# First projection group multiplied with x times scale alone, alpha in 16 products, later modulation rows behind the q and k group

## The chip, the core and the metric

The kernel runs on one NeuronCore of a Trainium2 chip. Time is device time in microseconds (us) of one execution; each kernel is run several times and the median stands for it. One further execution was recorded by the hardware profiler; its own time and trace are what the sections below read. Engines: PE (TensorE, matrix products; PEld is its weight load), DVE (VectorE), ACT (ScalarE), POOL (GpSimd), SP (SyncE, which issues most DMAs).

## What is computed

One decoder block on a sequence of 1024 tokens of width 1024, all in float32. Of it, this matters here:

```python
mod = silu(c) @ w_ada + b_ada                  # (6*1024), six rows of 1024
shift1, scale1, gate1, shift2, scale2, gate2 = split(mod, 6)
h = rms_norm(x, norm1_w) * (1 + scale1) + shift1
proj = h @ w_in                                # q, k, v, r, a_lr, su, sv, g_a, g_b
z = a_lr @ w_alpha_up + b_alpha                # a_lr: 16 columns of proj
log_a = log_sigmoid(z) / 16
o = gla_chunked(q, k, v, log_a)                # 4 heads, gated linear attention
...
x = x + gate1 * (merged @ w_out)
h2 = rms_norm(x, norm2_w) * (1 + scale2) + shift2
x = x + gate2 * peer(h2)                       # 8 heads, top 16 of 16384 experts
```

rms_norm divides each token's row by the root of its mean square. As that divisor belongs to a row (token) and shift1 to a column (channel) of h, a product of h with a weight matrix can also be made as: row divisor times (x * norm1_w * (1 + scale1)) @ w, plus shift1 @ w.

## The kernel before

The sequence is worked in two halves of 512 tokens. In each half h stands transposed in SBUF (channels on partitions, eight blocks k of 128), and the columns of w_in are taken in groups of 512: V0 and V1 (the values), QK0 and QK1 (queries and keys of two heads each), then SV0, SV1, R0, R1, A0, A1, SU0, SU1, B0, B1. A group is eight steps k; one step multiplies four blocks of 128 into four PSUM banks (`mm`). To keep float32 accuracy, a factor is split in a high part rounded to the fast type (`wh`, `hTh`, by ACT) and the rest (`wl`, `hTl`, by DVE), and a product is three fast ones: high by high, high by low, low by high, 12 per step. A product of unsplit float32 tiles (`whole`, tiles `xt` and `wt`) takes four slower ones instead.

What comes first is written by hand in `first_group` (L1218): each instruction is put behind the one before on its engine by `put` (L1088), so PE, DVE, ACT and SP have a fixed order there. SP loads x transposed (2 MB), then for each pair of blocks (2 k and 2 k + 1) the shift and scale columns of w_ada (2 MB a pair, `AdaCols` L1117) and two weight tiles. The row norm comes from ACT squares of the x tiles, DVE sums, a product with ones, POOL's power (L1262), and a product that spreads it over the partitions (`dg`, `rrow`). The modulation columns of a pair are eight tiles times silu(c), summed on DVE (`adc`, 512 wide: shift and scale, 256 each), and a product with ones sums them over partitions (`close`); `store` adds the bias (`mod`) and makes `scol` = (1 + scale) * norm1_w. Then ACT and DVE make hTh, the whole h block and hTl, and PE multiplies block ka split and kb whole. `alpha` (L1303) makes the 16 columns of a_lr in three products a block, 24 in all; four heads' decay products follow (L1483), with ACT's Abs, Exp and Ln and a scan on DVE (L1576). Products with ones or iota (`keep_warm`) fill PE's waits at the start.

All later groups go through `stream` (L1398), which loads and splits weights ahead (`weights_ahead`, four split pairs and five loaded tiles at most), and after each step pumps queues of side work at given rates (`step`, L1047). Queue `qa` holds the modulation rows for gate1, scale2, shift2 and gate2 (`ada_row` L1161): eight loads of 512 KB each and eight DVE sums of width 1024 (`adacc`), and a product. They start with V1. Outside the hand-ordered part, a scheduler that works on a simulated timeline decides how these streams are interleaved on each engine.

The second half computes h in `x_prep` and `h_split`, runs the same groups, and beside them the expert rows of the first half, gathered by POOL (`direct_rows`); the expert mixer for the rest ends the program.

Of the kernel before, what the change touches and what calls it, by code (L numbers as in the profile page):

```python
# [17 lines left out]
P = 128  # L18
# [29 lines left out]
RD = 0.62  # L48
UVC = 4
# [18 lines left out]
DIRECT = ((3,), (), (), ())  # L68
WARM = 10
YA = True  # L70
VV = (0, 1)
# [10 lines left out]
def block_kernel(ctx: ExitStack, tc: tile.TileContext, x, xT, cT, w_ada, b_ada, b_adaT, n1T, w_inp, w_alr,  # L82
# [972 lines left out]
    with ExitStack() as pa:  # L1055
# [23 lines left out]
        wal = b2.tile([RANK, 512], F32, name="wal", tag="b2")  # L1079
        walr = b2.tile([P, KD, RANK], F32, name="walr", tag="b2")  # L1080
        wst = s1.tile([P, 8, P], F32, name="wst")
        walr_h = g1.tile([P, KD, RANK], F32R, name="walr_h")
        walr_l = g1.tile([P, KD, RANK], F32R, name="walr_l")
        wal_h = g1.tile([RANK, 512], F32R, name="wal_h")
        wal_l = g1.tile([RANK, 512], F32R, name="wal_l")
        tail = {}

        def put(eng, fn, *args, **kw):  # L1088
            with tc.issue_after(tail[eng]) if eng in tail else nullcontext():
                tail[eng] = getattr(getattr(nc, eng), fn)(*args, **kw).ins  # L1090

# [13 lines left out]
        def ada_acc(c):  # L1105
            acc = t4("adacc")
            for k in range(KD):
                wt = t4("wada")
                nc.sync.dma_start(wt, w_ada[k * P:(k + 1) * P, c * D:(c + 1) * D])
                if k == 0:  # L1110
                    with tc.issue_after(hlast[1]):
                        nc.vector.tensor_scalar(acc, wt, sc[:, 0:1], None, op0=OP.mult)
# [4 lines left out]
        class AdaCols:  # L1117
            def __init__(self, kp):
                w2 = 2 * P
                self.kp, self.direct = kp, DIRECT[kp]  # L1120
                self.chain = [q for q in range(KD) if q not in self.direct]
                self.acc = gl.tile([P, 2, w2], F32, name="adc", bufs=3)
                self.ps = auxt([P, 2, 2])
                self.wa = []
                for q in range(0, KD, 2):
                    wa = t4("wada").rearrange("p (a c f) -> p a c f", a=2, c=2)
                    src = w_ada[q * P:(q + 2) * P, :].rearrange("(a p) n -> p a n", p=P)
                    for c in range(2):
                        put("sync", "dma_start", wa[:, :, c], src[:, :, c * D + kp * w2:c * D + (kp + 1) * w2])
                    self.wa += [wa[:, 0], wa[:, 1]]  # L1130
# [87 lines left out]
        def first_group(src, evac, aps):  # L1218
# [27 lines left out]
            for k in range(KD):  # L1246
                sq = rowp.tile([P, HALF], F32, name="sq", tag="row") if k else acc
                put("scalar", "activation", sq, xts[k], AF.Square)
                if 0 < k < KD - 1:
                    keep_warm(sq[:, 0:256])  # L1250
# [659 lines left out]
```

## Time and profile before

| | us |
|---|---|
| median of 3 runs | 1421.45 |
| lowest and highest | 1417.21, 1423.58 |
| profiled execution, its own time | 1415.31 |
| its span in the trace | 1413.3 |
| first product of V0 | 22.8 |
| first product of V1 | 58.25 |
| first product of QK0 | 85.99 |

The span runs from the first to the last recorded instruction; the execution's own time has about 2 us more. A profile row of a timeline gives start, length, engine, line, operation, tiles written and read, count, and in brackets the idle time of the engine before it with what ended it. A row of windows gives, for a stretch, the busy time of PE, PEld, DVE, ACT and POOL, then PE's granted clock as a share of 2.4 GHz, the busy share of the 16 DMA engines, and GB/s. Most instructions of the hand-ordered part stand at L1090, the line in `put`.

### The profile page before, as it was taken

The page shows a single profiled execution, that of the slowest core. Times are in us where ns is not written, and L with a number is a line of the kernel's source. Part 1 is how long each engine was busy: PE and PEld are TensorE (multiplying, and loading weights), DVE is VectorE, ACT ScalarE, POOL GpSimd, SP SyncE. Part 2 cuts the span into 40 slices and gives each one's busy share as a digit, 9 for nine tenths or more (in the row PEclk, how much of TensorE's full clock was granted, in tenths as well). Part 3 has the DMA queues.
Part 4 walks back from the last instruction along what each step waited for, and adds up shares of the span by engine and source line. Part 5 has one row for each costly group of instructions (what it writes and reads, how often), then busy time and mean ns, then how long its engine had stood idle before and what let it go on. Part 6 is the DMA issues. An engine that isn't in the chain of part 4 may idle for free.

```text
span 1413.3 us, 19480 instructions
## 1 busy us (share of the span) xinstructions
PE 1341.5 (95%) x5998; PEld 1030.9 (73%) x5998; DVE 1078.9 (76%) x3073; ACT 697.7 (49%) x1560; POOL 293.8 (21%) x271
## 2 busy tenths in 40 slices
PE   8999999999999899998989999999989999789996
PEld 6678877888888887676767888887768886445553
DVE  7785777434468678898879887779889877799785
ACT  4454343333345465475434566556546554545542
POOL 0100001000000121332443143311121133443321
PEclk9999999999999999999999999999999999999998
DMA  9753553332257475767687798897687668897984
GB/s 327 257 205 112 187 177 128 98 98 82 95 180 269 159 275 172 244 219 258 197 297 272 243 338 335 319 336 266 217 298 280 213 246 323 339 385 310 391 295 175
DMA packets 118243, 339.75 MB, mean 240 GB/s; under 512 B 14745, under 2 KB 24217, under 8 KB 106098
## 3 DMA queue, kind: packets, MB, share of 16 engines
q0 software_dynamic: 31488, 163.85, 31.5%
q1 hardware_dynamic: 69296, 129.24, 27.1%
q10 hardware_dynamic: 17346, 45.34, 8.9%
q8 instruction: 48, 0.79, 0.2%
q14 instruction: 65, 0.53, 0.1%
HBM read 314.15 MB, written 24.23 MB: 239 GB/s over the span
## 4 chain that ended last, share of the span: by engine, by line
PE 34%; DMA 7%; DVE 7%; issue 6%; ACT 2%; POOL 1%; DVEq 0%; ACTq 0%; POOLq 0%
PE acc L608 6%; PE mm L183 5%; PE mm L184 5%; PE mm L186 5%; DMA uvd<-in_down_dram,dix 3%; PE mm L189 2%; DMA uv<-in_tab_dram,dix 2%; PE mm L190 2%; PE mm L191 2%; DVE uv L582 1%; PE hps L580 1%; PE hps L581 1%; PE acc L628 1%; PE acc L627 1%; DMA uv<-in_tab_dram,ix 1%
## 5 line engine op out<-in xcount | busy, mean ns | idle before, releaser
L1385 ACT ACTIVATE wh<-wt 128x512 fp32r<-128x512 f32 x344 | 212.5, 627 | 284.0 <-PE mm L184 126.9
L1387 DVE TENSOR_TENSOR wl<-wt,wh 128x512 fp32r<-128x512 f32 x344 | 231.5, 685 | 125.8 <-PE mm L186 62.5
L183 PE MATMUL mm<-wh,hTh 128*128 128x512 f32 x648 | 255.7, 395 | 1.5 <-ACT wh L1385 1.5
L184 PE MATMUL mm<-wh,hTl 128*128 128x512 f32 x648 | 253.8, 392 | 0.0
L186 PE MATMUL mm<-wl,hTh 128*128 128x512 f32 x648 | 204.1, 397 | 2.4 <-DVE wl L1387 2.4
L183 PEld LDWEIGHTS mm<-wh,hTh 128*128 128x128 f32 x648 | 121.7, 188 | 30.6 <-issue 3.1
L186 PEld LDWEIGHTS mm<-wl,hTh 128*128 128x128 f32 x648 | 120.6, 188 | 30.3 <-DVE wl L1387 4.4
L184 PEld LDWEIGHTS mm<-wh,hTl 128*128 128x128 f32 x648 | 121.7, 188 | 25.8 <-issue 0.4
L527 POOL DMA_INDIRECT uv<-in_tab_dram,ix x74 | 82.5, 1114 | 274.0 <-ACT ix L559 134.0
L183 PE MATMUL mm<-hTh,wh 128*128 128x512 f32 x240 | 95.6, 398 | 0.0
L184 PE MATMUL mm<-hTl,wh 128*128 128x512 f32 x240 | 94.8, 395 | 0.0
L582 DVE SCALAR_TENSOR_TENSOR uv<-uv,hps 128x512 f32<-128x512 f32 x112 | 74.9, 680 | 22.9 <-DMA uv<-in_tab_dram,ix 16.4
L189 PE MATMUL mm<-wh,hTh 128*128 128x512 f32 x216 | 85.4, 403 | 1.9 <-ACT vt L1451 1.6
L190 PE MATMUL mm<-wl,hTh 128*128 128x512 f32 x216 | 86.2, 399 | 0.0
L191 PE MATMUL mm<-wh,hTl 128*128 128x512 f32 x216 | 85.8, 397 | 0.0
L189 PE MATMUL mm<-hTh,wh 128*128 128x256 f32 (+1 forms) x208 | 70.2, 340 | 7.8 <-DVE q L1521 5.7
L754 POOL DMA_INDIRECT uvd<-in_down_dram,dix x32 | 39.0, 1218 | 161.2 <-DVE ts L361 48.0
L186 PE MATMUL mm<-hTh,wl 128*128 128x512 f32 x240 | 71.4, 398 | 0.1
L190 PE MATMUL mm<-hTl,wh 128*128 128x256 f32 (+1 forms) x208 | 68.5, 331 | 3.0 <-DVE hTl L175 3.0
L620 DVE SCALAR_TENSOR_TENSOR vl<-uv,r,vh 128x512 fp32r<-128x512 f32 x82 | 60.1, 745 | 11.5 <-ACT vh L619 5.8
L191 PE MATMUL mm<-hTh,wl 128*128 128x256 f32 (+1 forms) x208 | 67.5, 332 | 0.0
L608 PE MATMUL acc<-uv,W 128*128 128x512 f32 x132 | 63.4, 602 | 2.3 <-ACT W L597 1.8
(957 smaller groups left out, 2896.1 us busy)
## 6 DMA issues: line engine op xcount, KB each, us to landing
wt<-in_w_inp_dram SPq DMA_DIRECT2D x224, 256.0 KB, 3.9
wt<-in_w_qp_dram SPq DMA_DIRECT2D x72, 256.0 KB, 3.9
wada<-in_w_ada_dram SPq DMA_DIRECT2D x32, 512.0 KB, 4.8
wt<-in_w_outp_dram SPq DMA_DIRECT2D x56, 256.0 KB, 3.4
wada<-in_w_ada_dram SPq DMA_DIRECT2D x32, 256.0 KB, 5.9
s_d<-so ACTq DMA_DIRECT2D x28, 256.0 KB, 5.9
xr<-in_x_dram ACTq DMA_DIRECT2D x8, 512.0 KB, 4.3
x_d<-x ACTq DMA_DIRECT2D x8, 512.0 KB, 5.1
```

The costliest lines, as they stand in the source:

```text
L183: nc.tensor.matmul(ps, lh, rh, start=False, stop=False)
L184: nc.tensor.matmul(ps, *((lh, rl) if feat else (ll, rh)), start=False, stop=False)
L186: nc.tensor.matmul(ps, *((ll, rh) if feat else (lh, rl)), start=False, stop=False)
L189: nc.tensor.matmul(ps, lh, rh, start=first, stop=False)
L190: nc.tensor.matmul(ps, lh, rl, start=False, stop=False)
L191: return nc.tensor.matmul(ps, ll, rh, start=False, stop=last).ins
L527: nc.gpsimd.indirect_dma_start(out=dst[:], out_offset=None, in_=src, in_offset=off)
L582: nc.vector.scalar_tensor_tensor(uv[0][:, sl], uv[0][:, sl], 1.0, hps, op0=OP.mult, op1=OP.mult, accum_out=r[:, 2 + n:3 + n])
L608: ins = nc.tensor.matmul(acc[:, sl], W, v[:, sl], start=first, stop=last).ins
L620: nc.vector.scalar_tensor_tensor(vl, v, r[:, 5:6], vh.bitcast(F32), op0=OP.mult, op1=OP.subtract)
L1385: nc.scalar.activation(wh, wt, AF.Identity)
L1387: nc.vector.tensor_tensor(wl, wt, wh.bitcast(F32), op=OP.subtract)
```

## The change

The first two groups of the first half become one hand-ordered part, `first_groups`. V0 is multiplied from x times `scol` alone: no norm, no shift. Scale columns come pair by pair (256 wide, four steps q), from a new input `w_asc` that is laid out so that a partition's piece is 4 KB; block 2q is multiplied whole, block 2q + 1 split. The row norm comes from x loaded by rows (`xb`, another 2 MB) and enters as a factor when V0's banks are copied out (`ev_v0`). The shift's part of V0 is made later: DVE sums V0's kept weight tiles times the shift columns (`shift_rows`, tile `so`), one product with ones sums it over partitions (`shift_sum`), and DVE adds it to the four value tiles (`shift_add`), at steps 1 to 7 of QK0. The shift columns come in two parts of 512 (`w_ash`); the first is needed to start V1, the second for V1's fifth block. V1 is multiplied with the complete h: `turn` brings the norm into the scaled x, `split_h` adds the shift and splits.

Alpha takes high and low weights as 32 columns of one tile (`walr2`), so a block needs two products instead of three, in both halves; it is made in V1 instead of V0. Two heads' decay follows V1, the other two stand behind QK0's first step, and ACT's Exp and Ln with them. The modulation rows start with QK1 at rates 1.0 (QK1), 1.25 (SV0, SV1), 0 (R0), 0.5 (R1), 1.0 (A0, A1). The tiles of x, V0's weights and rows of x stand in buffers of later tiles: V0's weights in the `row` buffers and in `wst`, so the loads of glw, lnw, lnb and wst on ACT's queue wait for the shift rows.

```diff
         def ada_acc(c):
-            acc = t4("adacc")
+            acc, wts = t4("adacc"), []
+
+            def load(k):
+                wts.append(t4("wada"))
+                nc.sync.dma_start(wts[k], w_ada[k * P:(k + 1) * P, (c - 2) * D:(c - 1) * D])
...
+        def alpha(aps, k, emit):
+            hi = aps, walr2[:, k], hTh[:, k], k == 0, k == KD - 1
+            lo = aps[:RANK], walr2[:, k, :RANK], hTl[:, k], False, False
+            for o, w, h, first, last in (lo, hi) if k == KD - 1 else (hi, lo):
+                ins = emit("tensor", "matmul", o, w, h, start=first, stop=last)
...
+            scs = [load_scale(0, v4)]
+            load_x(0, 1)
+            load_w(0, 1, whole=False)
+            scs.append(load_scale(1, v4))
+            load_x(2, 3)
+            load_w(2, 3)
+            scs.append(load_scale(2, b4))
+            load_x(4, 5)
+            load_w(4, 5)
...
+            def scaled(dst, k):
+                put("scalar", "activation", dst, xts[k], AF.Identity, scale=scol[:, k:k + 1])
...
+            def norm():
+                rstd = sm_p.tile([P, BH], F32, name="rstd")
+                rstd0.append(rstd)
+                put("vector", "tensor_scalar", rstd, ss, 1.0 / D, EPS, op0=OP.mult, op1=OP.add)
+                nc.gpsimd.tensor_tensor(rstd, rstd, mhalf[:, :BH], op=OP.pow)
...
+            def turn(k):
+                if k % 2:
+                    put("vector", "scalar_tensor_tensor", xts[k], xts[k], scol[:, k:k + 1], rrow, op0=OP.mult, op1=OP.mult)
+                else:
+                    put("vector", "tensor_tensor", xts[k], xts[k], rrow, op=OP.mult)
...
+            for q in range(4):
+                ka, kb = 2 * q, 2 * q + 1
+                nps, _, add, close = channel_sums(scs[q + 1], [], 2 * P) if q < 3 else channel_sums(shs[0], [], 512)
+                whole(pss, ka)
+                if q == 3:
+                    squares(2)
+                add(1)
+                if q < 3:
+                    nwh = high(wts[kb + 2])
+                    if q == 2:
+                        squares(0)
+                    add(KD)
+                    if q:
+                        scaled_low(kb)
+                    nwl = low(wts[kb + 2], nwh)
+                else:
+                    add(2)
+                    norm()
+                    scaled_low(kb)
+                    add(2)
+                    norm_rows(norm_spread())
+                    add(KD)
+                cut = (8, 4, 4, 12)[q]
+                order = by_bank if q == 3 else by_part
+                products(pss, kb, wh, wl, order[:cut])
+                close()
+                products(pss, kb, wh, wl, order[cut:])
...
+                if q < 3:
+                    store_scale(nps, q + 1)
+                    scaled(xts[kb + 1], kb + 1)
+                    scaled(hTh[:, kb + 2], kb + 2)
...
             for k in range(KD):
...
+                    turn(k)
+                    nwh = high(w1[k])
+                split_h(k)
+                if k:
+                    nwl = low(w1[k], nwh)
...
+                if k < 4:
+                    add(2)
+                order = by_bank if k in (0, KD - 1) else by_part
+                products(pss1, k, nwh, nwl, order[:8])
+                if k == 3:
+                    close()
+                products(pss1, k, nwh, nwl, order[8:])
...
+                group(w_inp[G_QK0], ev_qk(0), True, post={0: later_decays, **late_shift}, hold=hold)
+                for c, r in ((2, 0), (4, 1), (3, 2), (5, 3)):
+                    qa.add(ada_row(c, r))
...
+            rate["a"] = RSV
...
+            for gid, ev, ra in ((G_R0, ev_r(0), 0.0), (G_R1, ev_r(1), 0.5), (G_A0, ev_a(0), 1.0), (G_A1, ev_a(1), 1.0)):
+                rate["a"] = ra
```

PE, ahead of the first products and through the first pair, before (tile `xt` is x, `aux` and `gaux` are PSUM banks for side products):

```order
L1090 MATMUL aux<-dg,ones 128x512
L1090 MATMUL gaux<-iota,ones 128x256 x3
L1090 MATMUL aux<-ones,adc 128x1 x4
L1090 MATMUL gaux<-iota,ones 128x256 x2
L1090 MATMUL mm<-wh,hTh 128x512 x4
L1090 MATMUL mm<-wl,hTh 128x512 x4
L1090 MATMUL mm<-wh,hTl 128x512 x4
L1090 MATMUL mm<-wt,xt 128x512 x4
```

and with the change, at the same place (`w_235` holds weight blocks 0 and 1):

```order
L1088 MATMUL aux<-sc,wada 128x1 x8
L1088 MATMUL aux<-ones,adc 128x1 x2
L1088 MATMUL gaux<-iota,ones 128x256
L1088 MATMUL mm<-w_235,xt 128x512 x4
L1088 MATMUL mm<-wh,hTh 128x512 x4
L1088 MATMUL mm<-wl,hTh 128x512 x4
```

and in the last pair of V0 (`wst` holds weight blocks 6 and 7):

```order
L1088 MATMUL mm<-wh,hTl 128x512 x4
L1088 MATMUL mm<-wst,xt 128x512 x4
L1088 MATMUL aux<-dg,ones 128x512
L1088 MATMUL mm<-wh,hTh 128x512
L1088 MATMUL mm<-wl,hTh 128x512
```

The spread of the norm (`aux<-dg,ones`) stood ahead of all products; now it stands between the last pair's whole and split products, and the first accumulating product follows the first pair's two scale columns.

DVE in the last pair of V0 and up to V1's first block, with the change (`adc` are shift sums, `rstd` the norm, `dg` its diagonal):

```order
L1088 SCALAR_TENSOR_TENSOR adc<-wada,sc,adc 128x512 x2
L1088 TENSOR_SCALAR rstd<-ss 128x4
L1088 SCALAR_TENSOR_TENSOR hTl<-xt,scol,hTh 128x512
L1088 SCALAR_TENSOR_TENSOR adc<-wada,sc,adc 128x512 x2
L1088 TENSOR_TENSOR dg<-ident,rstd 128x512
L1088 SCALAR_TENSOR_TENSOR adc<-wada,sc,adc 128x512 x3
L1088 TENSOR_TENSOR xt<-xt,rrow 128x512
L1088 TENSOR_TENSOR mod<-aux,badat 128x4
```

Before, DVE had the norm at the very start:

```order
L1090 TENSOR_TENSOR sqa<-sqa,sq 128x512 x7
L1090 SCALAR_TENSOR_TENSOR adc<-wada,sc,adc 128x512
L1090 TENSOR_SCALAR rstd<-aux 128x4
L1090 SCALAR_TENSOR_TENSOR adc<-wada,sc,adc 128x512 x2
L1090 TENSOR_TENSOR dg<-ident,rstd 128x512
```

Norm and diagonal moved behind the first shift sums, whose tiles SP loads after all of V0's.

ACT during QK0, with the change (`vt` the value tiles, `za` the decays):

```order
L1564 ACTIVATE vt<-mm 128x512 x3
L452 DMA glw<-in_gla_w_dram 128x1024
L1564 ACTIVATE vt<-mm 128x512
L1497 ACTIVATE wh<-wt 128x512
L1088 ACTIVATE za<-gaux,balt 128x512 x2
L452 DMA lnw<-in_ln_w_dram 128x1024
L1497 ACTIVATE wh<-wt 128x512
L452 DMA lnb<-in_ln_b_dram 128x1024
L1088 ACTIVATE za<-gaux,balt 128x512 x2
L1609 ACTIVATE za<-za 128x512 x4
```

The three row loads stand among V1's copies and the decays of QK0's time; before they were issued during V0, ahead of these.

More of the change, by code (lines that the diff above doesn't have):

```diff
@@ L1161, in ada_row, with mod_products @@
+        def mod_products(ps, wa, rows, direct):
+            w = wa[0].shape[1] // P
+            for r in rows:
+                for j in range(w):
+                    put("tensor", "matmul", ps[:, j:j + 1], wa[r][:, j * P:(j + 1) * P], sc[:, r:r + 1],
+                        start=r == direct[0] and j == 0, stop=len(direct) == KD and r == direct[-1] and j == w - 1)
         def ada_row(c, r):
@@ new lines, in low, with whole, parts, products @@
+            def low(w, wh):
+                wl = wsp.tile([P, 512], F32R, name="wl")
+                put("vector", "tensor_tensor", wl, w, wh.bitcast(F32), op=OP.subtract)
+                return wl
+            def whole(pss, k):
+                for i, cs in enumerate(cuts):
+                    put("tensor", "matmul", pss[i], xts[k][:, cs], wts[k], start=k == 0, stop=False)
+            def parts(k, wh, wl):
+                return (hTh[:, k], wh), (hTh[:, k], wl), (hTl[:, k], wh)
+            def products(pss, k, wh, wl, todo):
+                for n, i in todo:
+                    a, w = parts(k, wh, wl)[n]
+                    put("tensor", "matmul", pss[i], a[:, cuts[i]], w, start=k == 0 and n == 0, stop=k == KD - 1 and n == 2)
@@ new lines, in first_groups @@
+            keep_warm(ones, WARM)
+            ps, prod, add, close = channel_sums(scs[0], [0, 1, 2, 3], 2 * P)
+            prod([0, 1, 2, 3])
+            add(KD)
+            close()
+            store_scale(ps, 0)
+            keep_warm(iota)
+            pss = [mm.tile([P, 512], F32, name="mm", tag="mm") for _ in range(4)]
+            scaled(xts[0], 0)
+            wh = high(wts[1])
+            scaled(hTh[:, 1], 1)
+            wl = low(wts[1], wh)
+            scaled_low(1)
+            xb, shs = [], []
@@ L1246, in first_group @@
+            split_const(walr, walr2[:, :, :RANK], walr2[:, :, RANK:])
+            keep0.extend(wts)
+            nps, _, add, close = channel_sums(shs[1], [], 512)
+            pss1 = [mm.tile([P, 512], F32, name="mm", tag="mm") for _ in range(4)]
             for k in range(KD):
[L1247 to L1250, printed above, removed]
@@ L1472, in block_kernel, with decays @@
+            if hf == NHALF - 1:
+                qdir.add(direct_rows(t4, range(DIR)))
+            aps = gauxt([2 * RANK, HALF])
+            last_z = []
+            def decays():
+                for fn, kw in ((AF.Exp, {"scale": -1.0}), (AF.Ln, {"bias": 1.0})):
+                    with tc.issue_after(zi[0]):
+                        for za in zas:
+                            zi[:] = [nc.scalar.activation(za, za, fn, **kw).ins]
+                zlast[:] = [zi[0]]
             alh = t2("alh", F32R)
```

437 lines of the change are left out of this document (229 added, 208 removed).

## The prediction

> **What bounds the kernel now.** I read the page first, then windows of ten microseconds, then the timelines of PE, DVE and ACT for the first 110 us, which is where the change stands.
>
> ```profile
> span 1413.3 us, 19480 instructions
> ...
> PE 1341.5 (95%) x5998; PEld 1030.9 (73%) x5998; DVE 1078.9 (76%) x3073; ACT 697.7 (49%) x1560; POOL 293.8 (21%) x271
> ```
> ```profile
> 30.00:40.00 10.00, 9.20 (x38) 5.51 (x38) 9.15 (x17) 4.29 (x6) 0.00 (x0) 1.00 1.06 332
> ...
> 300.00:310.00 10.00, 10.00 (x46) 8.29 (x45) 3.83 (x6) 3.04 (x6) 0.00 (x0) 1.00 0.24 79
> ```
> ```profile
> 100.00:420.00 320.00, 317.87 (x1475) 260.77 (x1474) 178.66 (x304) 113.48 (x213) 9.12 (x5) 1.00 0.39 130
> 420.00:740.00 320.00, 297.17 (x1470) 243.85 (x1469) 262.16 (x824) 169.32 (x334) 89.27 (x70) 0.98 0.68 231
> ```
>
> In the windows the columns are busy PE, weight load, DVE, ACT, POOL, then granted clock, DMA share and GB/s. From 100 to 420 us PE is busy 317.87 of 320 us: whatever PE gains before 100 us goes through that stretch undiminished. Before 60 us PE is not the bound, DVE is (9.15 of 10). The PE timeline shows its pace (start, length, engine, line, tiles, idle before):
>
> ```profile
> 22.79 1.20 PE L1090 MATMUL mm<-wh,hTh 128*128 128x512 f32 x4 [0.33 <-ACT hTh L1090]
> ...
> 25.64 3.59 PE L1090 MATMUL mm<-wt,xt 128*128 128x512 f32 x8
> 28.68 0.79 PE L1090 MATMUL gaux<-hTh,walr_h 128*16 128x512 f32 x1
> ...
> 30.21 1.05 PE L1090 MATMUL aux<-ones,adc 128*128 128x1 f32 x8 [0.28 <-DVE adc L1090]
> ...
> 41.92 1.19 PE L1090 MATMUL mm<-wh,hTh 128*128 128x512 f32 x4 [0.57 <-ACT hTh L1090]
> ...
> 51.28 1.20 PE L1090 MATMUL mm<-wh,hTh 128*128 128x512 f32 x4 [0.58 <-ACT hTh L1090]
> ...
> 58.02 0.39 PE L1090 MATMUL gaux<-hTh,walr_l 128*16 128x512 f32 x1
> 58.25 0.39 PE L189 MATMUL mm<-wh,hTh 128*128 128x512 f32 x1
> ...
> 84.18 1.88 PE L1171 MATMUL aux<-adacc,ones 128*1 128x512 f32 x4
> 85.99 0.50 PE L189 MATMUL mm<-hTh,wh 128*128 128x512 f32 x1
> ```
>
> The first product of V0 starts at 22.79, pairs follow every 9.36 us (41.92 to 51.28), V0 with alpha ends at 58.25, V1 with the four decay products at 84.18, and QK0 starts at 85.99 behind a modulation row's 1.88 us. Twelve split products take 2.85 us (22.79 to 25.64), so one takes 0.23; four unsplit ones take 3.04 (25.64 to 28.68), and closing a pair's column sums (30.21, eight passes) 0.9.
>
> **The change, part by part.**
>
> **Start.** Norm and shift leave the path; what is left is one scale column pair.
>
> ```profile
> 0.79 4.38 SPq L1090 DMA_DIRECT2D xt<-in_xT_dram  x8
> ...
> xt<-in_xT_dram SPq DMA_DIRECT2D x8, 256.0 KB, 3.8
> ```
> ```profile
> L1607 DVE SCALAR_TENSOR_TENSOR ot<-ot,rso,glw 128x256 f32<-128x256 f32 x32 | 13.4, 474 | 0.1
> ```
> ```profile
> L1090 ACT ACTIVATE adc<-wada,sc 128x512 f32<-128x512 f32 x4 | 2.9, 716 | 1.6 <-DMA wada<-in_w_ada_dram 1.6
> ```
> ```profile
> 26.26 3.90 DVE L1090 SCALAR_TENSOR_TENSOR adc<-wada,sc,adc 128x512 f32<-128x512 f32 x5
> ```
> ```profile
> 31.69 0.81 ACT L1090 ACTIVATE hTh<-xt,mod,scol 128x512 fp32r<-128x512 f32 x1 [4.51 <-DVE scol L1090]
> ```
>
> Issued at 0.79 and landing in 3.8, the first scale tile is there at about 4.6, the second (512 KB more) at 5.2. A sum over 512 columns that needs the one before takes 0.78 (3.90 by 5). At 256 columns the trace has no such chain: it lies between 0.40, half of that, and 0.78; I take 0.51, nearest to the 0.474 that one such instruction lasts. So: ACT's first sum 0.5 (0.716 at twice the width), three DVE sums 1.5, closing products 0.5 (half of the 0.9), bias and scale 0.4, scaling x 0.75 (the 0.81 row without its bias), hand-offs 0.2: the first product at **9.1** instead of 22.8.
>
> **Pairs.** A pair now goes round one chain: scaling x and its high part 1.5, first sum 0.5, seven sums 3.6, two DVE instructions put between the sums and the scale (hTl, wl; below) 1.3, bias and scale 0.3: **7.2 us**, above PE's 3.04 + 2.72 + 0.5. Pair 3 starts at 9.1 + 3 × 7.2 = 30.7, not 51.28: 20.6 us ahead.
>
> **What is given back before V1.** In pair 3 PE does its unsplit products (to 33.8), then stands at the row-norm product, which the code puts ahead of the split ones.
>
> ```profile
> L1198 ACT ACTIVATE xb<-xb 128x1024 f32<-128x1024 f32 x4 | 4.2, 1056 | 2.7 <-DMA xb<-in_x_dram 2.7
> ```
> ```profile
> 13.14 1.51 POOL L1262 TENSOR_TENSOR rstd<-rstd,mhalf 128x4 f32<-128x4 f32 x1 [10.45 <-DVE rstd L1090]
> ```
>
> ACT: hTh to 31.5, two squares of 1.06 to 33.6, the first shift sum to 34.3. DVE: two shift sums, queued ahead of the norm, to 35.9; POOL's power to 37.5, beside which DVE has two more shift sums queued, to 38.0; the diagonal to 38.7. So PE is idle **4.9 us**. Then 0.76 for the spread, 2.72 split products, 0.9 closing the shift sums, 0.2 its store, 0.75 hTh: V1's first product at 44.4, against 58.25.
>
> This needs 12.9 MB landed by about 37 us (scales 4.2, x and its rows 4.2, V0's weights 2.1, two small loads 0.3, shifts 2.1):
>
> ```profile
> 28.00:30.00 2.00, 1.93 (x6) 0.48 (x4) 1.93 (x3) 0.00 (x0) 0.00 (x0) 1.00 1.10 355
> ...
> 70.00:72.00 2.00, 2.00 (x10) 1.67 (x9) 2.00 (x3) 0.63 (x1) 0.00 (x0) 1.00 1.02 408
> 72.00:74.00 2.00, 2.00 (x10) 1.65 (x10) 2.00 (x4) 0.00 (x0) 0.00 (x0) 1.00 1.03 414
> ```
>
> Rows of 1 KB moved at 355 GB/s, 4 KB rows beside weights at 408 to 414. The new tensors are read in 4 KB rows, x and some weights in 2 KB; I take 10.0 MB at 400 and 2.9 at 355, 33.2 us, from 2.5 on: the last shift tile is there at 36, just in time. At 355 throughout it is 39, and V1 starts 1.3 us later. The Trainium skill ("DMA: Bandwidth & Descriptors", Specifications) sets HBM's limit for a core near 358 GB/s. The rows at 408 and 414 say otherwise for stretches of 2 us; by the page the sum would be those 1.3 us worse.
>
> **V1.**
>
> ```profile
> 97.83 1.27 DVE L1387 TENSOR_TENSOR wl<-wt,wh 128x512 fp32r<-128x512 f32 x2
> ```
>
> At some 0.63 for a 512-column DVE instruction (two in 1.27), each of V1's first four rows costs DVE a turn, hTl, wl and two shift sums, 3.3 us, with a wait for ACT's hTh (0.72) inside, so about 3.9, more than PE's 2.72 + 0.45 of alpha. After the fourth stand the second shift columns' closing (0.9), their store, splitting the decay weights (1.0), a turn and hTh, 2.9 us in all before PE goes on. Rows five to eight run near PE's pace, 3.3. With two heads' decay products (six, 1.4): 15.6 + 2.9 + 13.1 + 1.4 = 33.0 us, to **77.4**. Before, 58.25 to 84.18 held all four heads' decay.
>
> **QK0.**
>
> ```profile
> 78.18 1.15 ACT L1493 ACTIVATE za<-za 128x512 f32<-128x512 f32 x2
> ...
> 80.90 1.28 ACT L1496 ACT_TABLE_LOAD   x1
> ```
> ```profile
> 87.07 1.22 DVE L1576 TENSOR_TENSOR_SCAN G<-smask,za 128x512 f32<-128x512 f32 x1
> ```
> ```profile
> L1114 DVE SCALAR_TENSOR_TENSOR adacc<-wada,sc,adacc 128x1024 f32<-128x1024 f32 x28 | 35.8, 1280 | 16.5 <-DMA wada<-in_w_ada_dram 16.4
> ```
>
> Add the other two decays (six products, 1.4) and the shift's column sum 0.76: 79.5, against 85.99 − 1.88 = 84.1 (the modulation row only moves). Lead 4.6 us. Eight shift rows (5.2 us) and four additions (2.5) on DVE are hidden by QK0's 21.8 us of PE; eight modulation sums of 1.28 leave it. On ACT four row loads now wait for tiles that these shift rows release, with the decay's Exp and Ln and the weight splits queued behind; three to four split weights are ahead, so I take 0; without that cover it is the second rival.
>
> **Modulation rows.** 32 sums on DVE and their loads go behind QK0 and into the gates. The 300:310 row has DVE at 3.83 of 10 there: nothing.
>
> **Alpha** in the second half: 8 products of 0.23, **1.8 us**, if PE is the limit there (297 of 320 busy): between 0 and 1.8, I take all.
>
> **The clock** is the term that I cannot settle.
>
> ```profile
> 12.00:14.00 2.00, 2.00 (x15) 1.95 (x14) 1.54 (x3) 0.20 (x1) 0.86 (x1) 0.78 1.10 347
> 14.00:16.00 2.00, 2.00 (x6) 1.64 (x6) 1.52 (x3) 0.00 (x0) 0.65 (x1) 0.50 1.08 366
> ...
> 18.00:20.00 2.00, 2.00 (x5) 1.21 (x5) 0.12 (x2) 1.19 (x3) 0.00 (x0) 0.51 1.10 347
> ...
> 642.00:644.00 2.00, 0.00 (x0) 0.00 (x0) 2.00 (x9) 1.62 (x3) 0.87 (x1) 1.00 1.02 392
> 644.00:646.00 2.00, 1.02 (x3) 0.86 (x4) 2.00 (x7) 1.51 (x3) 0.28 (x1) 0.65 1.03 407
> 646.00:648.00 2.00, 2.00 (x6) 1.61 (x5) 2.00 (x7) 0.77 (x2) 0.00 (x0) 0.50 1.03 408
> 648.00:650.00 2.00, 2.00 (x10) 1.60 (x10) 2.00 (x8) 0.02 (x1) 0.00 (x0) 1.00 0.89 344
> ```
>
> After some four microseconds with little on PE the grant fell to 0.50 (1.2 GHz); about 3 us of products then went at that level, a loss of 1.5. At the kernel's start it stayed there from 13 to 20, a loss near 3.5. The change has two such places: the one-column products ahead of the first pair, and the 4.9 us at the norm. Between 0 and 5.2 us; I take 2.9. The Trainium skill ("TensorE: Matmul & The Clock Gate", What's actually happening) calls the throttled state the default that activity releases, and the 644 to 648 rows agree; by it both places start slow, 2.3 us worse than my value.
>
> **Sum.** 4.6 − 2.9 + 1.8 = 3.5 us. The profiled execution, 1415.31 with a span of 1413.3, becomes 1411.8; it lies 6.1 under the median of the runs, 1421.45, so the median becomes **1418.0**.
>
> **Rivals.**
>
> *The whole front comes through.* If 256-column sums run at 0.40, a pair takes 6.4 and pair 3 starts at 28.3; if the norm's wait then shrinks to 2 us, V1 starts near 39 and, at PE's own 25.4 + 1.4, ends near 66 to 68, with the clock high. Lead 11 or so, with alpha 13: 1408.5. For it speaks that PE had 20.6 us in hand at pair 3; against it stand DVE's sums queued ahead of the norm.
>
> *ACT stands at its row loads (slower).* If shift rows run late, ACT sits in front of Exp and Ln. Then eight of them at 0.55 and two table changes of 1.3, 7 us, come after the last shift row instead of beside QK0, and the scans (4 × 1.2) behind them; QK0's fifth and later weights wait too. 7 + 4.9 less some 3 of cover, 9 us: 1427. It decides once ACT waits longer than the 5 us of split weights ahead. Against it: DVE frees the tiles within 10 us of V1's end.
>
> *Nothing arrives.* The second half waits for gathers:
>
> ```profile
> 592.48 5.93 DMA uvd<-in_down_dram,dix
> ```
>
> These are issued from results of the first half, so they move with it; but if the altered order of instructions lengthens a wait there by the same 3 us, 1421.5.
>
> **How the numbers follow.** Forecast (1412 to 1424, a small gain or none) 0.53; whole front 0.27; ACT's loads or slow clock throughout 0.13; nothing 0.07. 0.5% is 7.1 us, about what a measurement of this kernel tells from no change. Faster by more: 0.27, same 0.60, slower 0.13. The range takes in most of the first rival and the slower one: 1408.5 to 1427.
>
> **What would show it.** Right: PE's first accumulating product near 9, pair starts 7.2 apart, a PE wait of 4 to 6 us for `dg`, V1's rows 0 to 3 about 4 us apart with DVE releasing PE, QK0 starting 2 to 5 us earlier than 85.99 less 1.88, low clock grants near 10 and 40 us. Wrong: pairs at 6 us, no wait at the norm, or ACT idle at a row load in QK0 for over 5 us; also any change of over 4 us between 100 us and the end that the start doesn't explain.

## The result: 1.1% slower

| | before | after |
|---|---|---|
| median of the runs, us | 1421.41 (4 runs, 1417.21 to 1423.58) | 1437.95 (4 runs, 1431.43 to 1439.08) |
| ratio | | 1.0108, 95% interval 1.0075 to 1.0141 |
| profiled execution, us | 1415.31 | 1431.43 |

The page of the changed kernel, its span and busy times:

```profile
span 1429.6 us, 19379 instructions
...
PE 1338.7 (94%) x5952; PEld 1027.3 (72%) x5952; DVE 1085.0 (76%) x3094; ACT 694.2 (49%) x1561; POOL 291.5 (20%) x270
```

PE has 2.8 us less to do than before and the span is 16.3 us longer: PE stands 90.9 us instead of 71.8. Where? First the front, the PE timeline of the changed kernel (start, length, engine, line, tiles, count, idle before):

```profile
10.22 4.79 PE L1088 MATMUL mm<-w,xt 128*128 128x512 f32 x8 [0.28 <-ACT xt L1088]
...
18.87 3.70 PE L1088 MATMUL mm<-w,xt 128*128 128x512 f32 x8 [0.40 <-ACT xt L1088]
...
26.00 3.60 PE L1088 MATMUL mm<-w,xt 128*128 128x512 f32 x8
...
40.83 2.05 PE L1088 MATMUL aux<-dg,ones 128*128 128x512 f32 x2 [4.32 <-DVE dg L1088]
41.89 1.42 PE L1088 MATMUL mm<-wh,hTh 128*128 128x512 f32 x1
...
47.26 0.95 PE L1088 MATMUL aux<-ones,adc 128*128 128x1 f32 x8
49.39 0.50 PE L1088 MATMUL mm<-wh,hTh 128*128 128x512 f32 x1 [1.18 <-ACT hTh L1088]
...
83.22 0.51 PE L188 MATMUL mm<-hTh,wh 128*128 128x512 f32 x1
```

The pairs, the wait for `dg` and the stages stand where the prediction had them, each somewhat late; QK0 starts at 83.22. Six decay products and the shift's sum (1.4 + 0.76) are still to come, so this stands for 85.4, against 84.1 before: the front loses 1.3 us. (That alone is within one execution's scatter: e13 below has before's front, and QK0 started at 83.52 in it, not at 85.99.) Then the copies of two later groups on ACT, before: the last of the first half (`sg`, group B1) and the last of the second half's query groups (`qt`); what follows is the stretch that ends the program.

```profile
395.55 0.60 ACT L1633 ACTIVATE sg<-mm 128x512 f32<-128x512 f32 x1
...
1209.03 0.59 ACT L1749 ACTIVATE qt<-mm 128x512 f32<-128x512 f32 x1
```

The same with the change (the fourth of the four merged `qt` copies starts at 1217.7):

```profile
401.68 0.60 ACT L1798 ACTIVATE sg<-mm 128x512 f32<-128x512 f32 x1
...
1215.68 2.67 ACT L1916 ACTIVATE qt<-mm 128x512 f32<-128x512 f32 x4 [0.29 <-PE mm L190]
```

So the 16.3 us arise in three places: **6.1** in the first half (1.3 of them ahead of QK0, 4.8 behind), **2.6** from there to the last query group, although alpha saves time there, and **7.6** in the last stretch (211.9 us instead of 204.3), where the edit changes nothing. Two thirds of the loss stand behind the first half, where the change's one edit is alpha, a saving.

### The profile page after: what moved, and what is told of

It reads as the page before. It is cut to its first block, busy times and chain, and to the rows that moved or that the text cites. A ratio compares the mean times of both kernels' runs of the same rounds, so it can differ in the third digit from the quotient of the medians.

```text
span 1429.6 us, 19379 instructions
## 1 busy us (share of the span) xinstructions
PE 1338.7 (94%) x5952; PEld 1027.3 (72%) x5952; DVE 1085.0 (76%) x3094; ACT 694.2 (49%) x1561; POOL 291.5 (20%) x270
## 5 line engine op out<-in xcount | busy, mean ns | idle before, releaser
L1497 ACT ACTIVATE wh<-wt 128x512 fp32r<-128x512 f32 x336 | 207.8, 627 | 280.8 <-PE mm L183 116.2
L1499 DVE TENSOR_TENSOR wl<-wt,wh 128x512 fp32r<-128x512 f32 x336 | 227.2, 689 | 109.2 <-ACT wh L1497 58.1
L182 PE MATMUL mm<-wh,hTh 128*128 128x512 f32 x624 | 246.0, 394 | 2.1 <-ACT wh L1497 2.1
L183 PE MATMUL mm<-wh,hTl 128*128 128x512 f32 x624 | 245.7, 394 | 0.0
L185 PE MATMUL mm<-wl,hTh 128*128 128x512 f32 x624 | 194.5, 395 | 2.2 <-DVE wl L1499 2.2
L182 PEld LDWEIGHTS mm<-wh,hTh 128*128 128x128 f32 x624 | 117.4, 188 | 28.8 <-ACT wh L1497 3.1
L185 PEld LDWEIGHTS mm<-wl,hTh 128*128 128x128 f32 x624 | 116.0, 188 | 29.6 <-DVE wl L1499 3.0
L183 PEld LDWEIGHTS mm<-wh,hTl 128*128 128x128 f32 x624 | 117.2, 188 | 25.1 <-issue 0.9
L188 PE MATMUL mm<-wh,hTh 128*128 128x512 f32 x208 | 84.0, 410 | 4.7 <-DVE x L1886 2.1
L190 PE MATMUL mm<-wh,hTl 128*128 128x512 f32 x208 | 81.8, 393 | 0.0
L189 PE MATMUL mm<-wl,hTh 128*128 128x512 f32 x208 | 81.7, 393 | 0.0
```

What stands on the lines that cost most here:

```text
L182: nc.tensor.matmul(ps, lh, rh, start=False, stop=False)
L183: nc.tensor.matmul(ps, *((lh, rl) if feat else (ll, rh)), start=False, stop=False)
L185: nc.tensor.matmul(ps, *((ll, rh) if feat else (lh, rl)), start=False, stop=False)
L188: nc.tensor.matmul(ps, lh, rh, start=first, stop=False)
L189: nc.tensor.matmul(ps, lh, rl, start=False, stop=False)
L190: return nc.tensor.matmul(ps, ll, rh, start=False, stop=last).ins
```

## The experiments

The table holds all kernels: end of the first half (start of its last `sg` copy), from there to the last `qt` copy, the last stretch (three parts of the profiled span), and the ratio of the runs to before's with its interval. "Order" names the second half's order of instructions: the scheduler makes one of a few, which I compared row by row on each engine. X is before's, Z the changed kernel's; "own" was seen once. "Shift" is explained at the thirteenth run.

| run | order | shift | first half | to last query | last stretch | ratio (95%) |
|---|---|---|---|---|---|---|
| before | X | no | 395.6 | 813.4 | 204.3 | 1 |
| after | Z | yes | 401.7 | 816.0 | 211.9 | 1.0108 (1.0075 to 1.0141) |
| e1 | Y | no | 398.2 | 810.7 | 202.6 | 1.0028 (1.0000 to 1.0056) |
| e2 | Y | no | 397.3 | 813.1 | 205.0 | 1.0033 (1.0008 to 1.0058) |
| e3 | own | yes | 406.8 | 817.4 | 210.3 | 1.0104 (1.0066 to 1.0141) |
| e4 | Y, some 50 rows off | yes | 395.1 | 810.9 | 211.4 | 1.0034 (1.0010 to 1.0058) |
| e5 | Y | no | 397.2 | 817.0 | 203.8 | 1.0042 (1.0012 to 1.0072) |
| e6 | X | no | 403.4 | 814.4 | 204.6 | 1.0010 (0.9989 to 1.0030) |
| e7 | V | yes | 403.4 | 809.0 | 209.4 | 1.0045 (1.0021 to 1.0070) |
| e8 | Z | yes | 404.7 | 817.6 | 210.7 | 1.0103 (1.0062 to 1.0144) |
| e9 | V | yes | 399.5 | 805.0 | 211.1 | 1.0029 (1.0001 to 1.0056) |
| e10 | Z | yes | 401.1 | 818.4 | 212.1 | 1.0124 (1.0048 to 1.0201) |
| e11 | Z | yes | 407.6 | 811.1 | 212.9 | 1.0159 (1.0093 to 1.0224) |
| e12 | own | yes | 398.1 | 811.7 | 213.9 | 1.0050 (1.0021 to 1.0079) |
| e13 | X | yes | 392.9 | 813.2 | 211.9 | 1.0023 (1.0000 to 1.0045) |
| e14 | Z | no | 401.2 | 824.4 | 203.0 | 1.0085 (1.0059 to 1.0110) |
| e15 | V | no | 404.2 | 806.7 | 201.7 | 1.0006 (0.9979 to 1.0033) |
| e16 | V | no | 398.5 | 807.7 | 202.8 | 0.9960 (0.9937 to 0.9983) |

One execution's first half varies by itself: e13's is 2.7 us shorter than before's, with the same rows. The parts are to be read over several kernels.

**Each edit alone.** e1 is before with alpha in 16 products, e2 before with the modulation rows moved (and loaded ahead as in the changed kernel):

```diff
-                    put("tensor", "matmul", aps, w[:, k], a[:, k], start=k == 0 and n == 0, stop=k == KD - 1 and n == 2)
+                alpha2(aps, k, put)
...
-                    alr = mm3(aps, walr_h[:, k], walr_l[:, k], hTh[:, k], hTl[:, k], k == 0, k == KD - 1)
+                    alr = alpha2(aps, k, plain)
```

> The kernel before, with only alpha in 16 products instead of 24, in both halves. If an edit costs what its own instructions cost: 8 products of 0.23 us fewer in the second half, none on the path in the first, so 1.8 us faster than before, 1419 to 1420. If the 14 us that the changed kernel loses between V1 of the second half and the end come from the alpha edit: about 1430. If they come from the order in which the scheduler puts the second half's instructions (it differs from before's here too, from V0 of the second half on): nothing up to V0 of the second half, and then a second half that is some us longer or shorter than before's with PE idle in other places, 1415 to 1432; the later run with the rows alone, whose second half has the same order, must then be off by the same amount.

```diff
+            if hf == 0:
+                for c, r in ((2, 0), (4, 1), (3, 2), (5, 3)):
+                    qa.add(ada_row(c, r))
+            rate["a"] = 1.25
             group(w_inp[G_SV0], ev_sv(0), False)
...
+            for gid, ev, ra in ((G_R0, ev_r(0), 0.0), (G_R1, ev_r(1), 0.5), (G_A0, ev_a(0), 1.0), (G_A1, ev_a(1), 1.0)):
+                rate["a"] = ra
```

> The kernel before, with only the modulation rows moved behind the first q and k group, at the changed kernel's rates. If the moved rows crowd DVE: PE waits of 2 to 5 us between 100 and 240 us that before doesn't have, R0 to A1 late by as much, 1423 to 1426. If the moved rows are hidden: no change up to the second half. On the theory of the order: the second half differs from before's by the same amount as in the run with alpha alone (without its 1.8 us).

Neither is the 1.1%. Both bring the second half into order Y. Alpha's saving doesn't show in e1's total (1.0028). What the edits do in their places: from the last query copy of the first half to the first head's copy of the second (558.4 to 662.5 in before), the five kernels with 24 alpha products took 103.0 to 105.5 us, e1 100.7 and the changed kernel 100.5, some 3.5 us less than before; all thirteen with 16 products took 99.0 to 101.3, whatever their order. Eight products of 0.23 are 1.8 of this; the other part is a wait ahead of V1's first product that is shorter or gone, here before's row:

```profile
591.18 0.50 PE L189 MATMUL mm<-wh,hTh 128*128 128x512 f32 x1 [1.63 <-ACT vt L1451]
```

The rows are not hidden. From QK0's first product to the end of the first half, before took 309.6 us. e2 took 315.0 (82.32 to 397.3), 313.1 without the one row's products that before has done by then: 3.5 us for the rows. The five kernels with before's rows (before, e1, e5, e6, e13) took 309.2 to 312.3 there, those with the changed front 315.4 to 320.8. The waits of PE between 84 and 242 us with the change (who, how long in all, times, longest):

```profile
PE mm L185 <- DVE wl L1499: 2.2, 2, 1.3
PE mm L188 <- DVE sg L1782: 1.4, 1, 1.4
PE mm L188 <- DVE q L1673: 0.8, 1, 0.8
PE mm L188 <- ACT svg L1548: 0.5, 1, 0.5
```

Before had one wait there, 2.1 us. The changed kernel's windows of 10 us show why (PE, weight load, DVE, ACT, POOL, grant, DMA share, GB/s):

```profile
220.00:230.00 10.00, 10.00 (x40) 6.74 (x40) 10.00 (x16) 1.90 (x3) 4.10 (x3) 1.00 0.68 217
230.00:240.00 10.00, 8.56 (x38) 6.73 (x38) 10.00 (x15) 3.54 (x6) 0.00 (x0) 1.00 0.56 179
```

DVE is full there, with the sums among the weight splits and copies that PE waits for.

**Rows earlier, norm earlier.** e3 is the changed kernel with the rows queued ahead of QK0 and the rates left at 1:

```diff
+                for c, r in ((2, 0), (4, 1), (3, 2), (5, 3)):
+                    qa.add(ada_row(c, r))
                 group(w_inp[G_QK0], ev_qk(0), True, post={0: later_decays, **late_shift}, hold=hold)
-            rate["a"] = RSV
-                rate["a"] = ra
```

> The changed kernel, with the modulation rows started with the first q and k group at rate 1 throughout, the nearest to their old place that its front allows. If crowding of DVE by the moved rows costs 3 to 4.6 us of the changed kernel's loss: 1433.5 to 1435, or slower where the sums meet the shift rows in the q and k group. If the rows are hidden: 1438. On the theory of the order, the second half is a fourth order of its own and may be anything between before's and the changed kernel's.

No gain: QK0's first product to the end of the first half took 319.2 us, against 318.5, so on this front the rows cost as much at either place. e4 moves the norm:

```diff
-                    add(2)
-                    norm()
                     scaled_low(kb)
-                    add(2)
-                    norm_rows(norm_spread())
+                    norm()
+                    add(1)
+                    dg = norm_spread()
                     add(KD)
+                if q == 3:
+                    products(pss, kb, wh, wl, order[:6])
+                    norm_rows(dg)
...
```

> The changed kernel, with the row norm and its diagonal ahead of the shift sums on DVE, and the spread of the norm behind half of the last pair's split products. If the front's lateness is this wait and the slow clock behind it: no PE wait over 1.5 us there, V1 from 44 to 45 instead of 49.4, QK0 4 to 6 us earlier than 83.2; if that goes through to the end, 1432 to 1434. If the second half's order decides the rest: its second half has the order of the two runs on before from R0 on, and takes as long as theirs, so that the total may be 1420 to 1428.

PE's timeline of e4:

```profile
37.58 1.02 PE L1088 MATMUL aux<-dg,ones 128*128 128x512 f32 x2
...
42.01 1.02 PE L1088 MATMUL aux<-ones,adc 128*128 128x1 f32 x8 [2.03 <-DVE adc L1088]
44.04 0.80 PE L1088 MATMUL mm<-wh,hTh 128*128 128x512 f32 x1 [1.01 <-ACT hTh L1088]
```

The wait for `dg` is gone, V1 starts at 44.04 instead of 49.39, and the first half ends 6.6 us earlier. That is more than the front had lost. But the last stretch stays at 211.4 us, and e4's total, 1.0034, isn't the front's alone: the way to the last query copy is 5.1 us shorter too, in order Y.

**The same work in another order.** e5 and e6 are before, e7 and e8 the changed kernel, with 4 or 8 products on PE whose result nothing reads, between the front and what follows; nothing else is changed:

```diff
             hlast[:] = [tail["scalar"], tail["vector"]]
+            keep_warm(iota, 4)
```

They shift the scheduler's timeline a little, and with it the order of the second half, hundreds of us later. The expectations priced them at 0.12 us each; by e5's PE row four took 1.89, some 0.47 each, and by e11's below 32 took 13.98, 0.44 each:

```profile
58.51 1.89 PE L1090 MATMUL gaux<-iota,ones 128*128 128x256 f32 x8
```

> The kernel before, with four idle products (128 x 256, some 0.12 us each) on PE between V0 and V1; nothing else is changed and no other work is added. The scheduler, whose simulated timeline shifts by this, puts the second half in another order than before's: the same one, engine by engine, as in the run with the moved rows alone. If the time depends on the work alone: before plus 0.5 us, ratio 1.0003. If it depends on the second half's order: before plus 0.5 plus what that order costs, which the runs with alpha alone and with the rows alone put at some 3 us: ratio 1.002 to 1.004; the milestones to the end of the first half then agree with before's within a microsecond, and the loss stands behind V1 of the second half.

> The same with eight idle products, 0.9 us. With eight the scheduler gives the second half the very order of before. So on both theories before plus 0.9 us, ratio 1.0006: the control to the run with four.

> The changed kernel, with four idle products on PE behind V1 (0.5 us). The second half comes in an order of its own, most of PE's rows as in before. If the work alone decides: the changed kernel plus 0.5 us, ratio to before 1.0112. If the second half's order costs the changed kernel 7 to 9 us: a ratio of 1.003 to 1.006 should this order be as good as before's, and anywhere else if it isn't; only a ratio of 1.009 to 1.013 speaks against the theory.

> The changed kernel with eight idle products behind V1 (0.9 us), with which the second half keeps the changed kernel's order in all but a dozen rows. On both theories the changed kernel plus 0.9 us, ratio to before 1.0108 to 1.0118; it is the control to the run with four, and a second measurement of what the changed kernel loses in the first half and in the second.

On the changed kernel four idle products make the program 0.58% faster than eight; 1.7 us, 0.12%, of this is the idle products' own price. So some 6.5 us are the order's, 11 if e7 is held against the changed kernel itself. (Percentages here are differences of the table's ratios. The medians of e7 and e8 lie 12.4 us apart.) On before, four cost 0.32% more than eight, though they take 1.7 us less; but there the medians lie only 1.1 us apart (1420.45, 1419.33) and the intervals overlap, so that order Y is slower than X is not shown.

e9 to e12 try this on other fronts. In e9, e10 and e12 the norm stands as in e4, two shift rows are summed by one-column products on PE, and 12, 16 and 1 idle products follow V1; e11 is the changed kernel with 32 idle products in the wait for `dg`:

```diff
-                nps, _, add, close = channel_sums(scs[q + 1], [], 2 * P) if q < 3 else channel_sums(shs[0], [], 512)
+                nps, prod, add, close = channel_sums(scs[q + 1], [], 2 * P) if q < 3 else channel_sums(shs[0], [6, 7], 512)
...
+                if q == 3:
+                    prod([6, 7])
...
+            keep_warm(iota, 12)
```
```diff
                 rps = auxt([P, HALF])
+                keep_warm(iota, 32)
                 put("tensor", "matmul", rps, ones, dg, start=True, stop=True)
```

> The changed kernel with a repaired front: the norm ahead of the shift sums as before in the run that moved it, two of the eight shift rows summed by one-column products on PE instead of on DVE; and twelve idle products behind V1 (1.4 us), with which the second half takes the order of the run with four idle products on the changed kernel. Front: no idle time over 1 us between the last pair and the closing of the shift sums, V1's first product near 43 with the grant at 1.00 behind it. End of the first half about a microsecond ahead of before's. If the second half's order is what else counts, it takes what it took in the run with four idle products: ratio to before 0.999 to 1.001. If the changed kernel's loss lay in its work: some 7 us less than the changed kernel, 1.005 to 1.006.

> The same with sixteen idle products (1.9 us), with which the second half has the order of the changed kernel, in all but some 50 rows. By the order: 6 to 9 us over the run with twelve, a ratio of 1.004 to 1.007, and the distance grows between the heads of the second half and the end. By the work: 0.5 us over it.

> The changed kernel with 32 idle products on PE in the wait for the norm's diagonal (3.7 of its 4.3 us); the second half's order stays. If the slow clock costs the front what its rows say (products 0.43 instead of 0.23 apart from 42 to 47 and through V1's first block): granted clock 1.00 from 40 to 56, V1's first product at 47 instead of 49.4, QK0's at 79.5 to 81 instead of 83.2, ratio to before 1.0085 to 1.0095. If DVE sets V1's pace anyway: V1 at 47, but QK0 at 82 to 83 and no change of the total.

> The repaired front with one idle product (0.1 us): the second half takes an order that differs from that of the run with twelve in some 280 of PE's rows, nearly all of them in the last quarter, and that no run has shown. If this order is as good: 1.3 us under the run with twelve, ratio to before 0.998 to 1.000, not to be told from no change. If the last quarter's order counts for much: off by several us either way.

e9 and e10 are one front with orders V and Z: 1.0029 and 1.0124, of which 0.0012 are four more idle products. Neither came as expected: e9 is between its two ranges, and e10 is 13.5 us over e9, not 6 to 9. The intervals overlap a little, but the runs don't: the slowest of e9's ten took 1422.55 us, the fastest of e10's four 1426.32. Over all kernels, the way from the first half's end to the last query took 805.0 to 809.0 us in order V (four kernels, mean 807.1) and 811.1 to 824.4 in order Z (five, mean 817.5). Windows over the groups SU0 to B0 of the second half, e9:

```profile
864.00:951.00 87.00, 87.00 (x417) 71.67 (x416) 68.86 (x180) 48.43 (x118) 22.68 (x21) 1.00 0.89 325
```

and e10:

```profile
870.00:966.00 96.00, 91.94 (x426) 72.63 (x425) 70.28 (x180) 48.60 (x119) 21.64 (x20) 1.00 0.85 307
```

In order V PE never stands in these groups. In Z they take 9 us longer: PE stands 4.1 us, in five waits, for `vh`, `vl`, `hh` of the expert work and for `us`, and it is busy 4.9 us longer, with nine matrix products more recorded in this stretch. How the rest of Z's loss comes about wasn't traced. e12's order, seen once, is no better than Y. The direct shift rows gave nothing: eight one-column products took 1.7 us on PE, V1 began at 44.78, and the grant still fell behind its first block (0.50 from 46 to 48 us).

e11 missed, since its idle products took 13.98 us in a wait of 4.3. It measures the clock all the same, by its PE timeline:

```profile
35.85 13.98 PE L1088 MATMUL gaux<-iota,ones 128*128 128x256 f32 x64
49.67 1.02 PE L1088 MATMUL aux<-dg,ones 128*128 128x512 f32 x2
50.12 0.80 PE L1088 MATMUL mm<-wh,hTh 128*128 128x512 f32 x1
...
53.30 0.95 PE L1088 MATMUL aux<-ones,adc 128*128 128x1 f32 x8
```

Behind a busy PE, at a grant of 1.00, the twelve split products took 3.2 us (50.12 to 53.30), in the changed kernel 5.4 (41.89 to 47.26): the slow clock costs 2.2 us there.

**What is left over of a rate.** All kernels with the changed front had 209 to 214 us in the last stretch, all with the old front 203 to 205, in any order. The suspect: queues of expert work are pumped at each step at rates of 0.84 and 0.62, and one unit is done when the sum reaches 1. The hand-ordered V1 takes its eight steps without `step()`, which shifts the remainders by 0.28 and 0.04 for good (the table's "shift"). e13 gives before that shift alone; e14 takes it from the changed kernel, e15 with four idle products besides, e16 with those on the repaired front:

```diff
             hlast[:] = [tail["scalar"], tail["vector"]]
+            qp.credit += 1 - KD * RP % 1
+            qdir.credit += 1 - KD * RD % 1
```
```diff
             hlast[:] = [tail["scalar"], tail["vector"]]
+            for _ in range(KD):
+                step()
```

> The kernel before, with nothing changed but the remainders of two counters: the queues of expert work are pumped at 0.84 and 0.62 a step, and the changed kernel's hand-ordered V1 takes 8 steps without pumping them, which shifts what is left over by 0.28 and 0.04 of a unit at every later step. Here the kernel before gets that shift. Only some 15 of PE's rows, 70 of DVE's, 90 of ACT's and 3 gathers change their place, all in the second half's last fifth. If this shift makes the stretch behind the last query group (209 to 214 us in every kernel with the changed front, 203 to 205 in every kernel with the old one) longer: 209 to 212 us there instead of 204.3, ratio to before 1.003 to 1.006. If that stretch depends on something else of the changed front: 203 to 205, ratio 1.000.

> The changed kernel, with the eight steps' pumping put back behind V1 (no work is queued then, so only the remainders change). The scheduler's order of the second half stays the changed kernel's but for the same few rows at its end. By the theory of the remainders: the last stretch 203 to 206 us instead of 211.9, ratio to before 1.004 to 1.008. Otherwise as the changed kernel, 1.0103 to 1.0124.

> The changed kernel with the pumping put back and the four idle products: the other order of the second half, and the remainders of before. If order and remainders are what the changed kernel loses behind its first half, 8 and 5 to 7 us of the 15: ratio to before 0.998 to 1.001, and the last stretch at 203 to 206 us. If the two are one cause and don't add: 1.004 to 1.005, as with the four idle products alone.

> The repaired front (norm ahead of the shift sums, two shift rows on PE) with the pumping put back and four idle products: the order of the run before it in this call, on a front that is 3 to 6 us earlier. If what the front gains goes through to the end: 3 to 5 us under that run, ratio to before 0.995 to 0.998. If the second half's waits take it up: as that run.

The last stretch of before, in windows:

```profile
1209.00:1413.30 204.30, 176.12 (x539) 94.53 (x539) 166.23 (x696) 100.75 (x319) 71.30 (x72) 0.95 0.81 313
```

of e13, the same program but for the remainders:

```profile
1206.10:1418.00 211.90, 174.22 (x543) 93.55 (x541) 167.69 (x698) 101.49 (x322) 74.71 (x71) 0.93 0.79 307
```

and of e14, the changed kernel without the shift:

```profile
1225.60:1428.60 203.00, 172.22 (x547) 91.73 (x545) 165.51 (x694) 100.97 (x319) 70.53 (x72) 0.97 0.82 318
```

PE has no more to do with the shift, it stands longer: 37.7 us of e13's stretch, 28.2 of before's. Over all 18 kernels the two sorts don't overlap: 201.7 to 205.0 without the shift, 209.4 to 213.9 with it. On POOL the shift changes which expert list is fetched into which buffers: `uvu` and `uvv` are a pair of tiles 1024 wide, `uv` one tile of 2048, `dix_1` and `dix_2` two lists. Before:

```
L527 DMA uvu<-in_down_dram,dix_1_137 128x1024
L527 DMA uv<-in_tab_dram,dix_1_137 128x2048
L527 DMA uvv<-in_up_dram,dix_1_137 128x1024
L527 DMA uvu<-in_down_dram,dix_2_138 128x1024
```

e13, at the same place:

```
L527 DMA uvu<-in_down_dram,dix_2_138 128x1024
L527 DMA uv<-in_tab_dram,dix_1_137 128x2048
L527 DMA uvv<-in_up_dram,dix_2_138 128x1024
L527 DMA uvu<-in_down_dram,dix_2_138 128x1024
```

By the ratios the shift is worth 3 to 6 us (e13 3.3, e14 against the changed kernel 3.3, e15 against e7 5.5), less than the 7 to 9 of the profiled stretches; why is open. e13's interval begins at no difference, so on before alone it is just short of shown, though e13's median lies 5.2 us over before's, measured beside it (1422.91, 1417.68). In before one `dix_1` list goes into the pair; in e13 a `dix_2` list does, the `dix_1` list goes into a wide `uv`, and the program has one gather less. Why this costs so much at the end wasn't tried. The plainest proof of the order is e14 against e15, four idle products apart: all seven runs of e14 (order Z, 1424.70 to 1434.86 us) are above all ten of e15 (order V, 1408.28 to 1422.91), and the medians lie 13.1 us apart. Together, order and remainders explain what was lost behind the first half: **e15, the change's own work untouched, stands at 1.0006** (0.9979 to 1.0033) against 1.0108. And with the front repaired as well, **e16 beats both kernels: 0.9960** (0.9937 to 0.9983), 5.7 us under before, with 1.9 us of idle products in it.

By the table's parts this is not the rewritten front's gain. e15 ends its first half 8.6 us later than before and gets that back behind: 6.7 us on the way to the last query copy, from alpha and from order V, which may be better than before's own, and 2.6 in the last stretch. The repair takes 5.7 us off the first half (e16 against e15, in the same order), but e16 still ends it 2.9 us later than before; its lead is 5.7 us on the way to the last query and 1.5 in the last stretch. No run has before's front with 16 alpha products in order V, so that the rewritten front earns anything is not shown.

## Why the prediction was wrong

Its forecast was 1418.0, the measurement 1437.95, above the range's end of 1427.0. The step that failed most is the second half: the prediction let it gain alpha's 1.8 us and put an altered order of instructions at nothing, or at one wait of 3 us, and the order and the shifted remainders of two queues cost some 14 us there. Next come the modulation rows, also put at nothing, and the front, which gave no lead. Step by step:

- **Start and pairs**: 9.1 forecast, 10.22 measured; pairs 8.65, 7.13 and 6.9 us apart instead of 7.2. The chain is right: ACT's scalings at its head start 6.94 apart (18.10, 25.04, 31.98). But PE fills these intervals too (9.88 of 10 us busy from 20 to 30), where the prediction had it at 6.3. The first interval is longer because ACT, and DVE behind it, waited for weight tiles to land, a wait that the sum didn't have:

```profile
11.22 0.63 ACT L1088 ACTIVATE wh<-w 128x512 fp32r<-128x512 f32 x1 [1.05 <-DMA w<-in_w_inp_dram]
...
16.44 0.63 ACT L1088 ACTIVATE wh<-w 128x512 fp32r<-128x512 f32 x1 [3.41 <-DMA w<-in_w_inp_dram]
```

- **The norm's wait**: 4.9 forecast, 4.32 measured, released by `dg`, behind the shift sums as the prediction had it.
- **The transfers**: the prediction took 400 GB/s. These windows of the changed kernel show it, and the clock:

```profile
36.00:38.00 2.00, 0.52 (x2) 0.00 (x0) 1.60 (x4) 0.33 (x1) 0.00 (x0) 1.00 1.05 405
38.00:40.00 2.00, 0.00 (x0) 0.00 (x0) 1.97 (x3) 0.00 (x0) 1.45 (x1) 0.94 1.03 408
40.00:42.00 2.00, 1.17 (x3) 0.68 (x3) 1.97 (x4) 0.00 (x0) 0.00 (x0) 0.50 1.02 404
...
48.00:50.00 2.00, 0.82 (x4) 0.42 (x4) 1.37 (x5) 2.00 (x5) 0.00 (x0) 1.00 0.01 4
50.00:52.00 2.00, 1.49 (x4) 1.16 (x4) 1.90 (x3) 0.53 (x2) 0.00 (x0) 0.50 0.40 131
```

They move 404 to 408 GB/s. The Trainium skill ("DMA: Bandwidth & Descriptors", Specifications) sets HBM's limit for a core near 358, as half of what two cores share. The kernel ran on one core and the trace shows more, so the price that this figure would have added was rightly left out.

- **The clock**: 2.9 us for two places. At the first pair (granted 0.88 from 10 to 20 us) the chain above set the pace, and PE had 0.40 us to spare. At the norm alone it was 2.2 (e11), and the grant fell once more, to 0.50 at 50 us, behind the stand at V1's first block. By the Trainium skill ("TensorE: Matmul & The Clock Gate", What's actually happening) the throttled state is the default that activity releases; the rows from 40 to 52 us, and the 1.00 behind e11's busy wait, agree.
- **V1 and QK0**: QK0 was to stand for 82.4 (79.5 and the clock's 2.9), it stood for 85.4. Of these 3.0 us 2.2 were lost up to pair 3 (32.92 instead of 30.7). (The terms that the prediction lists ahead of V1 add up to 44.0, not to its 44.4.) The front was 1.3 us behind before's instead of 1.7 ahead.
- **Modulation rows, "nothing"**: failed. They and the shift rows cost 4.8 us between QK0 and the first half's end, the rows alone 3.5 (e2). The cover was read at 300 to 310 us, where DVE was busy 3.83 of 10; but the sums run from 138 to 282, beside splits and copies, where DVE filled up to 10.00 of 10.
- **Alpha**: 1.8 forecast, about 3.5 measured; a wait behind it went too.
- **ACT's row loads** (the slower rival): ACT's longest wait from 80 to 110 us is 3.2, for `q`, none at a load. The 0 was right, the rival wrong.
- **"Whatever PE gains before 100 us goes through undiminished"**: true to the first half's end (e4 starts QK0 6.1 us earlier than the changed kernel and ends the half 6.6 earlier), and to the last query group where the order is the same: e6, late by 7.8 us at the first half's end, is late by 8.8 there.
- **"Nothing arrives"** held the actual cause, an altered order of instructions, but as one wait for a gather, at 3 us and a chance of 0.07. That is the step that failed most. The stretch with that gather got shorter (100.5 instead of 104.1 us, above); the altered order lost 6.2 us in the whole second half (2.6 measured, and alpha's gain that went with it), and the shifted remainders, for which the prediction had no term, 7.6 at its end. Its own sign of being wrong, a change of over 4 us behind 100 us that the start doesn't explain, came true.

The sum by the profiled executions: 1.3 + 4.8 − 3.6 + 6.2 + 7.6 = 16.3 us. The order's 6.2 is what is left over, not measured by itself: held against order V, order Z costs 10.4 us by the means, and 6.5 to 11 by the ratios of e7, e8 and the changed kernel.

## What to carry to other kernels

Where a scheduler orders the work on a simulated timeline, and queues run at fractional rates, an edit is not local: compare the program's order on every engine to its end, and count the steps that a rewritten stretch no longer pumps. An edit without work (a few idle products, a remainder) measures how much the rest depends on its order; only beyond that is a difference the edit's own. Among such edits a better order can be picked, as e15 and e16 show, but what it gains is then not the change's. Work that is moved is to be priced at the rows where it will run, not at the nearest idle one.

## What the hardware showed unasked

- An idle product of 128 x 256 in float32 takes 0.44 to 0.47 us at the full clock (13.98 by 32, 1.89 by 4), twice a split product of 512 columns (0.23).
- The DMA engines moved 400 to 406 GB/s in each of the three windows of 10 us from 10 to 40 us, in rows of 2 and 4 KB.
- One kernel's executions spread over some 1% (before: 1410.4 to 1424.3 in 25 runs), while the profiled last stretch of one order keeps to some 2 us.
